# A seven-product scheme for the down projection of two token blocks

## The chip, the cores and the metric

The kernel runs on one core of a Trainium2 chip. The metric is the device time of one execution in microseconds (us); the median of three runs is given. The engines are TensorE (PE: matmuls; PEld: its weight loads), VectorE (DVE), ScalarE (ACT), GpSimd (POOL) and SyncE (SP), whose queue issues nearly all DMAs.

## The reference

One decoder layer over 2048 tokens with model width 1024: a modulated norm, an input projection, forgetting attention beside a state-space group, an output projection with a gated residual; then a gated MLP with a causal convolution of width 3. Only the MLP matters here:

```python
D_FF = 2816
h = rmsnorm(x, g_ffn[l]) * (1.0 + sc_f) + sh_f
gate_pre, val = jnp.split(h @ w_up[l], 2, axis=-1)
gate_pre = causal_dwconv(gate_pre, conv_w[l], conv_b[l])
y = (jax.nn.silu(gate_pre) * val) @ w_down[l]
x = x + gt_f * y
return rmsnorm(x, g_final)
```

All inputs and outputs are float32.

## The kernel before

Tokens are worked on in four blocks of 512 (TB). Tensors lie transposed: 128 channels on the partitions, tokens along the free dimension. The hidden width of 2816 is cut into 22 rows of 128 (NFF), the model width into 8 tiles of 128. A float32 product is made of three matmuls in a reduced format: every operand is split into a high part (a cast on ScalarE, line 77 for weights) and a low part (a subtraction on VectorE, line 78), and high x high, low x high and high x low are added up in a PSUM bank.

Blocks 0 and 1 go through the MLP one by one. Blocks 2 and 3 go together, and for them the up projection already uses a seven-product scheme (Winograd's form of Strassen's): `up_pair(i)` computes row i of the gate and of the value for both blocks at once. The 2 x 2 shape is made of the two halves of the model width (inner), gate and value (outputs) and the two blocks. Its weight combinations s1 to s4 are computed on POOL (lines 1353 to 1358), its operands are in SBUF from earlier on, and its seven products accumulate in the PSUM banks X and Y (two buffers each) and Z (one). In the program's order: X takes b11, Y takes b21, Z takes t1; X then takes t2 on top, Z takes b22, X takes t3, a second Y takes t4. In between, copies (L1385, L1387, L1389, L1395) and additions (L1386, L1391, L1396, L1399) take the running sums out to gs (gate) and vz (value), which have two buffers each. Then come the convolution and SiLU over both blocks (L1403 to L1409, on cvt, gs and vz), and the result, 128 x 1024, is split into ah (L1412) and al (L1413) and written to DRAM by two DMAs (L1415). The tiles cvt, ah and al share four buffers with the tag "row".

`down_pair(b)` is then run for block 2 and for block 3. It goes twice over four outputs d with four accumulators in PSUM, over the 22 rows in the groups FFG = (6, 6, 5, 5). The parts of the first group's activations are loaded into buffers of the tag h (L1434), those of the other groups into tiles of their own (L1437), x1 (the residual) into the yt tiles (L1451). Weights come for each block anew through two raw buffers and three buffers for each of the parts. The matmuls are L1472 to L1474. After the last group each output is scaled by tf, added to x1 (L1424), squared (L333) and summed (L334). Block 2's norm (its scalings are L1492) is put six steps into block 3. In block 3 the last group's last four outputs are made in two halves of 256 tokens, each followed by `finish_last`: sums over the channels, an inverse root in small VectorE operations (L166 to L176), scalings on VectorE (L1516) and POOL (L1514), and the output's DMAs.

The order of the instructions in each engine's queue is set before the run by a planner with a cost model: among instructions whose inputs and buffers are ready in its model, the one that comes first in the program goes first. `tc.issue_after` puts instructions of a block behind a given one on its queue, and `tc.high_priority` moves a block forward. A pool hands out a buffer of a tag once the last reader of its previous content is done. Opening a pool where another was closed waits tile by tile.

Of the kernel before, what the change touches and what calls it, by code (L numbers as in the profile page):

```python
# [12 lines left out]
F32 = mybir.dt.float32  # L13
F32R = mybir.dt.float32r
# [3 lines left out]
ALU = mybir.AluOpType  # L18
# [28 lines left out]
NSC = 2  # L47

# [63 lines left out]
def hybrid_layer(ctx, tc, x, c_t, w_ada, b_col, gains, w_flat, bf_row, a_re, a_im, log_dt,  # L112
# [88 lines left out]
    act_d = [dt(f"act{i}", [2, P, 2, TB]) for i in range(NFF)]  # L201
# [1136 lines left out]
    def up_pair(i, ops, ups):  # L1338
# [71 lines left out]
        ah = row_pool["row"].tile([P, n], F32R, name="ah", tag="row", bufs=4)  # L1410
        al = row_pool["row"].tile([P, n], F32R, name="al", tag="row", bufs=4)
        A.copy(ah, vz)  # L1412
        V.tensor_tensor(out=al, in0=vz, in1=ah.bitcast(F32), op=ALU.subtract)  # L1413
        for j, a in enumerate((ah, al)):
            (A if i == NFF - 1 else Q).dma_start(act_d[i][:, :, j, :].rearrange("b p n -> p b n"),  # L1415
                        a.rearrange("p (b n) -> p b n", b=2).bitcast(F32))

    def down_pair(b, ap, dps, misc, tail):

        sq = sq_acc()  # L1420
        act, yt, step = [], [], 0

        def evict(d, ps, ts, eng):
            V.scalar_tensor_tensor(out=yt[d][:, ts], in0=ps[:, ts], scalar=mod["tf"][:, d : d + 1], in1=yt[d][:, ts],  # L1424
                                   op0=ALU.mult, op1=ALU.add)
            sum_squares(sq, d == 0, yt[d][:, ts], ts, eng)

        def load_act(g):
            c0 = sum(FFG[:g])
            for c in range(c0, c0 + FFG[g]):  # L1430
                if g == 0:
                    act.append(h_parts())
                    for j, t in enumerate(act[-1]):
                        Q.dma_start(t.bitcast(F32), act_d[c][b % 2, :, j])  # L1434
                else:
                    t = ap.tile([P, 2, TB], F32R, name="act", tag=f"act{c}", bufs=1)
                    Q.dma_start(t.bitcast(F32), act_d[c][b % 2])  # L1437
                    act.append((t[:, 0], t[:, 1]))

        load_act(0)  # L1440
        for half in range(2):
            ds = range(4 * half, 4 * half + 4)
            pss = {d: dps.tile([P, 512], F32, name="acc_ps", tag="acc", bufs=4) for d in ds}
            c0 = 0
            for g, n in enumerate(FFG):
                last = g == len(FFG) - 1
                if g == 2:
                    with tc.issue_after(weights.last.ins):
                        for d in ds:
                            t = ap.tile([P, TB], F32, name="yt", tag="yt", bufs=8)  # L1450
                            Q.dma_start(t, x1_d[b][d])  # L1451
                            yt.append(t)
                cut = tail and last and half == 1
                ws = {}
                for p in range(2 if cut else 1):
                    ts = slice(p * 256, (p + 1) * 256) if cut else slice(0, TB)
                    for d in ds:
                        if d not in ws:
                            so, sn = dn_slots[g][d]
                            own = [ap.tile([P, sn], F32R, name=f"w_{nm}", tag=f"cut_{nm}{d}", bufs=1)  # L1460
                                   for nm in ("hi", "lo")] if cut else (None, None)
                            ws[d] = weights.split(weights.raw(so, sn), sn, *own)
                        wh, wl = ws[d]
                        if half == 0 and d == ds[3] and not last:
                            with tc.issue_after(weights.last.ins):
                                load_act(g + 1)
                        for c in range(n):
                            ah, al = (t[:, ts] for t in act[c0 + c])
                            a, bb = wh[:, c * P : (c + 1) * P], wl[:, c * P : (c + 1) * P]
                            st = g == 0 and c == 0  # L1470
                            sp_ = c == n - 1 and (last or tail and half == 1 and g == len(FFG) - 2)
                            T.matmul(pss[d][:, ts], lhsT=a, rhs=ah, start=st, stop=False, skip_group_check=cut)  # L1472
                            T.matmul(pss[d][:, ts], lhsT=a, rhs=al, start=False, stop=False, skip_group_check=cut)
                            T.matmul(pss[d][:, ts], lhsT=bb, rhs=ah, start=False, stop=sp_, skip_group_check=cut)  # L1474
                            step += 1
                            if step == 6 and norm_late:
                                norm_late.pop()()
                        if last:
                            evict(d, pss[d], ts, V)
                    if cut:  # L1480
                        with tc.high_priority():
                            finish_last(b, yt, sq, p, misc)
                c0 += n
# [252 lines left out]
```

## Time and profile before

| | us |
|---|---|
| median of 3 runs | 2645.68 |
| lowest and highest | 2643.41, 2648.35 |
| the profiled execution | 2644.54 |
| its span, first to last instruction | 2642.8 |

Row 1 to row 21 of `up_pair` fill the time up to 2374.3 us, and the two calls of `down_pair` the rest. All times of the trace count from the start of the span. In the page's list of groups a row shows the line, the engine, the operation, output <- inputs, shape and count, then the busy time and the mean duration in ns, then the idle time of the engine before these instructions and what ended it. A timeline row starts with its start and its duration in us. In a row of waits stand: who waited for whom, us in total, times, the longest.

### The profile page before, as it was taken

What the parts mean: (1) busy time and instruction counts of PE and PEld (TensorE: products, weight loads), DVE (VectorE), ACT (ScalarE), POOL (GpSimd) and SP (SyncE); (2) the same over time, 40 slices, a digit from 0 to 9 for tenths busy, and PEclk for the clock granted to TensorE, in tenths of its full rate; (3) what the DMA queues carried; (4) which work ended last, traced back from release to release, by engine and by line L of the source; (5) the groups of instructions that cost most, each with busy time, mean ns of one, the idle gap of its engine ahead of it and who ended that gap; (6) DMA issues with size and microseconds to landing.
All of it is one profiled execution on the core that took longest, in us unless ns stands there. A gap on an engine that the chain in (4) does not pass through costs nothing.

```text
span 2642.8 us, 35640 instructions
## 1 busy us (share of the span) xinstructions
PE 2552.0 (97%) x12343; PEld 2066.4 (78%) x12343; DVE 1934.6 (73%) x3568; ACT 1237.3 (47%) x2056; POOL 184.2 (7%) x146
## 2 busy tenths in 40 slices
PE   6999999998999999999999999999989999999997
PEld 3888777887788888888778877888768888887876
DVE  7989588966887878886877767676598778773343
ACT  3423255553564545564645555565544444442222
POOL 0001000000000000000000000000034334320000
PEclk8999999999999999999999999999999999999999
DMA  8586987667466565655656555556623232346563
GB/s 300 165 267 209 293 266 211 201 195 239 144 205 214 188 200 165 204 176 201 198 184 223 178 191 172 184 173 248 223 91 120 102 121 97 118 162 246 173 229 100
DMA packets 265925, 500.63 MB, mean 189 GB/s; under 512 B 27120, under 2 KB 111984, under 8 KB 265744
## 3 DMA queue, kind: packets, MB, share of 16 engines
q1 hardware_dynamic: 263920, 493.10, 56.9%
q0 software_dynamic: 1280, 4.20, 0.4%
q8 instruction: 98, 1.61, 0.3%
q10 hardware_dynamic: 544, 1.05, 0.1%
q14 instruction: 83, 0.68, 0.1%
HBM read 371.17 MB, written 127.01 MB: 189 GB/s over the span
## 4 chain that ended last, share of the span: by engine, by line
PE 76%; DMA 8%; DVE 8%; issue 4%; ACT 1%; SPq 1%; POOL 0%; ACTq 0%; DVEq 0%; POOLq 0%
PE ff_ps L1248 18%; PE up_x L1371 7%; PE ff_ps L1222 6%; PE up_y L1371 4%; PE up_z L1371 4%; PE ff_ps L1280 3%; PE ff_ps L1282 3%; PE ff_ps L1281 3%; DMA wada<-in_w_ada 3%; PE o_ps L1008 2%; PE o_ps L1012 2%; PE qs_ps L462 2%; PE vq_ps L462 2%; DMA w_raw<-in_w_flat 2%; PE proj_ps L429 2%
## 5 line engine op out<-in xcount | busy, mean ns | idle before, releaser
L78 DVE TENSOR_TENSOR w_lo<-w_raw,w_hi 128x1024 fp32r<-128x1024 f32 (+2 forms) x219 | 235.6, 1077 | 204.7 <-ACT w_hi L77 202.7
L77 ACT CAST w_hi<-w_raw 128x1024 fp32r<-128x1024 f32 (+2 forms) x219 | 203.0, 929 | 359.1 <-DMA w_raw<-in_w_flat 109.0
L1248 PE MATMUL ff_ps<-h_lo,w_hi 128*128 128x512 f32 x704 | 279.4, 397 | 0.9 <-DVE h_lo L381 0.8
L1248 PE MATMUL ff_ps<-h_hi,w_lo 128*128 128x512 f32 x704 | 279.6, 397 | 0.0
L1248 PE MATMUL ff_ps<-h_hi,w_hi 128*128 128x512 f32 x704 | 279.2, 399 | 0.0
L999 DVE TENSOR_TENSOR pl<-pf,ph 128x512 fp32r<-128x512 f32 (+1 forms) x320 | 194.8, 618 | 18.6 <-ACT ph L998 17.6
L998 ACT CAST ph<-pf 128x512 fp32r<-128x512 f32 (+1 forms) x320 | 177.9, 569 | 61.5 <-PE o_ps L1008 55.6
L1007 DVE TENSOR_TENSOR acc<-acc,pf 128x512 f32<-128x512 f32 (+2 forms) x264 | 159.2, 604 | 28.6 <-ACT pf L997 26.0
L1248 PEld LDWEIGHTS ff_ps<-h_lo,w_hi 128*128 128x128 f32 x704 | 133.3, 189 | 29.8 <-DVE h_lo L381 1.4
L997 ACT ACTIVATE pf<-sc_ps 128x512 f32<-128x512 f32 (+2 forms) x184 | 98.4, 539 | 122.4 <-PE sc_ps L988 73.7
L1248 PEld LDWEIGHTS ff_ps<-h_hi,w_lo 128*128 128x128 f32 x704 | 133.1, 189 | 28.8
L1248 PEld LDWEIGHTS ff_ps<-h_hi,w_hi 128*128 128x128 f32 x704 | 133.2, 189 | 28.7 <-issue 0.2
L107 ACT CAST w_hi<-w_raw 128x1024 fp32r<-128x1024 f32 (+2 forms) x100 | 96.4, 964 | 104.1 <-PE ff_ps L1222 42.2
L1281 PE MATMUL ff_ps<-act_lo,w_hi 128*128 128x512 f32 x352 | 139.5, 397 | 0.0
L1280 PE MATMUL ff_ps<-act_hi,w_hi 128*128 128x512 f32 x352 | 139.3, 398 | 0.2 <-ACT rt L368 0.2
L1282 PE MATMUL ff_ps<-act_hi,w_lo 128*128 128x512 f32 x352 | 139.4, 397 | 0.0
L949 DVE TENSOR_REDUCE mx<-sc_ps 128x1 f32<-128x512 f32 (+2 forms) x164 | 97.5, 599 | 50.2 <-PE sc_ps L944 25.5
L1008 PE MATMUL o_ps<-ph,vv 128*128 128x512 f32 (+1 forms) x320 | 120.8, 378 | 1.7 <-ACT ph L998 1.7
L1371 PE MATMUL up_x<-hh,w_hi 128*128 128x512 f32 x352 | 112.7, 400 | 6.1 <-DVE hh L378 4.4
L1012 PE MATMUL o_ps<-pl,vv 128*128 128x512 f32 (+2 forms) x312 | 116.2, 374 | 0.9 <-DVE pl L999 0.9
L1472 PE MATMUL acc_ps<-act,w_hi 128*128 128x512 f32 (+1 forms) x276 | 105.0, 380 | 3.1 <-ACT w_hi L77 2.5
L1474 PE MATMUL acc_ps<-act,w_lo 128*128 128x512 f32 (+1 forms) x276 | 104.5, 380 | 0.4
(581 smaller groups left out, 6719.6 us busy)
## 6 DMA issues: line engine op xcount, KB each, us to landing
w_raw<-in_w_flat SPq DMA_DIRECT2D x193, 512.0 KB
w_lo<-wlo SPq DMA_DIRECT2D x68, 512.0 KB
wlo<-w_lo SPq DMA_DIRECT2D x52, 512.0 KB
w_raw<-in_w_flat SPq DMA_DIRECT2D x64, 384.0 KB
kb<-kb SPq DMA_DIRECT2D x80, 256.0 KB
vv<-v SPq DMA_DIRECT2D x80, 256.0 KB
w_raw<-in_w_flat SPq DMA_DIRECT2D x64, 320.0 KB
act<-act SPq DMA_DIRECT2D x32, 512.0 KB
```

Of the source, the lines that this page charges most:

```text
L77: nc.scalar.copy(hi[:, :n], raw[:, :n])
L78: nc.vector.tensor_tensor(out=lo[:, :n], in0=raw[:, :n], in1=hi[:, :n].bitcast(F32), op=ALU.subtract)
L998: A.copy(ph[:, cs], pf[:, cs])
L999: V.tensor_tensor(out=pl[:, cs], in0=pf[:, cs], in1=ph[:, cs].bitcast(F32), op=ALU.subtract)
L1007: eng.tensor_tensor(out=acc[j][:, cs], in0=acc[j][:, cs], in1=pf[:, cs], op=ALU.add)
L1008: T.matmul(o_ps[:, cs], lhsT=vt[:, i, :], rhs=ph[:, cs], start=first, stop=False)
L1012: T.matmul(o_ps[:, cs], lhsT=vt[:, i, :], rhs=pl[:, cs], start=False, stop=(b > 0 and ch == b - 1 and i == 3))
L1248: T.matmul(ps, lhsT=lt, rhs=rt, start=(n == 0), stop=(n == 23))
L1280: T.matmul(ps, lhsT=a, rhs=ah[:, ts], start=(c == 0), stop=False)
L1281: T.matmul(ps, lhsT=a, rhs=al[:, ts], start=False, stop=False)
L1282: mark[0] = T.matmul(ps, lhsT=bb, rhs=ah[:, ts], start=False, stop=(c == n - 1))
L1371: mark[0] = T.matmul(ps, lhsT=lt, rhs=rt, start=(first and n == 0), stop=(n == 11), skip_group_check=not first)
```

## The change

`down_pair` for two blocks becomes `down_both`. Rows 0, 1 (FIRST) and 18 to 21 (LAST) stay direct products, for both blocks. Rows 2 to 17 form eight row pairs in the groups JOINT of two, three and three pairs. For a group and a pair of outputs the 2 x 2 shape is: even and odd row (inner), the two outputs, the two blocks. Seven products replace eight, with the weight sums s1 to s4 made on VectorE from the raw weights of the two outputs, and with eight additions from PSUM into the outputs y, which are in SBUF for both blocks from the start. They are begun by the FIRST rows (copied out with the scale tf on ScalarE); x1 is added later.

The operands of the seven products (b11, b21, t1, t2, b22, t3, t4) are made in `up_pair`: an even row of a joint pair stores its block 2 part as b11 and keeps vz; the odd row makes four differences and six operands. Each operand is split into both parts in one tile and written with one DMA of 512 KB. In the down stage, operands, activations and x1 go through 27 buffers (ROOM: 9 of h, 6 on the right side, 12 in the pool "act"), filled in order of use as buffers come free, with a cap that rises from step to step (`state["room"]`).

```diff
+RING = 6
+RINGL = 12
+NHP = 9
+ROOM = NHP + RING + RINGL
+STEP = 3
+FIRST = (0, 1)
+LAST = (18, 19, 20, 21)
+JOINT = ((1, 2), (3, 4, 5), (6, 7, 8))
+KINDS = ("b11", "b21", "t1", "t2", "b22", "t3", "t4")
...
+        if i in act_d:
...
+            return
+        def operand(kind, f):
+            o = row_pool["row"].tile([P, 2, TB], F32R, name="op", tag="row", bufs=4)
+            A.copy(o[:, 0], f)
+            V.tensor_tensor(out=o[:, 1], in0=f, in1=o[:, 0].bitcast(F32), op=ALU.subtract)
+            Q.dma_start(op_d[i // 2][kind], o.bitcast(F32))
+        def comb(a, b, to):
+            V.tensor_tensor(out=to, in0=a, in1=b, op=ALU.subtract)
+            return to
+        if i % 2 == 0:
+            operand("b11", va)
+            even[0] = vz
+            return
+        b11, b12 = even[0][:, 0:TB], even[0][:, TB : 2 * TB]
+        c13, c24 = (row_pool["row"].tile([P, 2, TB], F32, name="c", tag="row", bufs=4) for _ in range(2))
+        t1 = comb(b12, b11, c13[:, 0])
+        t3 = comb(vb, b12, c13[:, 1])
+        t2 = comb(vb, t1, c24[:, 0])
+        t4 = comb(va, t2, c24[:, 1])
+        for kind, f in (("b21", va), ("t1", t1), ("t2", t2), ("b22", vb), ("t3", t3), ("t4", t4)):
+            operand(kind, f)
...
+        for d in range(8):
+            w = weights.split(w_cols(0, n, d), n * P)
+            for b in (2, 3):
+                ps = bank(next(banks))
+                plain(ps, w, first[b])
+                t = rp.tile([P, TB], F32, name="yt", tag=f"yt{b}{d}", bufs=1)
+                y[b].append(t)
+                A.activation(t, ps, AF.Copy, scale=tf[:, d : d + 1])
+            state["room"] = min(state["room"] + STEP, 4 + 7 * len(JOINT[0]))
+            with tc.issue_after(weights.last.ins):
+                fill()
...
+                s12, s1, s2 = pair("s12")
+                s_op(s1, a21, a22, ALU.add)
+                s_op(s2, s1, a11, ALU.subtract)
+                w12 = weights.split(s12, 2 * n * P)
+                s43, s4, s3 = pair("s43")
+                s_op(s4, a12, s2, ALU.subtract)
+                s_op(s3, a11, a21, ALU.subtract)
+                w43 = weights.split(s43, 2 * n * P)
+                A.copy(hv, a22)
+                V.tensor_tensor(out=lv, in0=a22, in1=hv.bitcast(F32), op=ALU.subtract)
+                w22 = (hi, lo)
...
+                X, Y, Z = bank("x"), bank("y"), bank("z")
+                product(X, wa, 0, 2 * P, "b11")
+                product(Y, wa, P, 2 * P, "b21")
+                add(2, d1, X)
+                product(Z, w12, 0, P, "t1")
+                add(2, d1, Y)
+                add(3, d2, Z)
+                product(X, w12, n * P, P, "t2", False)
+                add(3, d1, X)
+                product(Z, w43, 0, P, "b22", False)
+                add(3, d1, Z)
+                product(X, w43, n * P, P, "t3", False)
+                add(2, d2, X)
+                add(3, d2, X)
+                Y2 = bank("y")
+                product(Y2, w22, 0, P, "t4")
+                add(2, d2, Y2)
+                if g == len(JOINT) - 1 and dp:
+                    for d in range(4):
+                        add_x1(*((2, d), (2, d + 4), (3, d))[dp - 1])
...
+                with tc.high_priority():
+                    norm_late.append(norm_of(2, y[2], sq, misc))
+            else:
...
+                norm_late[0](range(8))
...
```

In the last pass of a group (dp = 3) the buffers of each product's operands are given to the next group's loads. Block 2's scalings now stand in the program ahead of block 3's two halves. X, Y and Z have two PSUM banks each in the down stage.

More of the change, by code (lines that the diff above doesn't have):

```diff
@@ L200, in hybrid_layer @@
     x1_d = {b: [dt(f"x1_{b}_{d}", [P, TB]) for d in range(8)] for b in (2, 3)}
-    act_d = [dt(f"act{i}", [2, P, 2, TB]) for i in range(NFF)]
+    act_d = {i: dt(f"act{i}", [2, P, 2, TB]) for i in FIRST + LAST}
+    op_d = {j: {k: dt(f"op{j}{k}", [P, 2, TB]) for k in KINDS} for js in JOINT for j in js}
     off = 0
@@ L1409, in up_pair @@
         V.scalar_tensor_tensor(out=vz, in0=t, scalar=0.5, in1=vz, op0=ALU.mult, op1=ALU.mult)
[L1410 to L1434, printed above, removed]
-                else:
[L1436 to L1447, printed above, removed]
-                    with tc.issue_after(weights.last.ins):
[L1449 to L1483, printed above, removed]
-        if not tail:
-            ps = misc()
-            token_sums(ps, sq, 0, 4)
-            r = rsqrt_mean(ps[:, 0:4], 4, D)
-            def norm():
-                rt = spread(r, misc)
-                for d in range(8):
-                    V.scalar_tensor_tensor(out=yt[d], in0=yt[d], scalar=gain[:, 24 + d : 25 + d], in1=rt,
-                                           op0=ALU.mult, op1=ALU.mult)
-                    Q.dma_start(out[b, d], yt[d])
-            norm_late.append(norm)
@@ new lines, in up_pair @@
+        if i in act_d:
+            ah = row_pool["row"].tile([P, n], F32R, name="ah", tag="row", bufs=4)
+            al = row_pool["row"].tile([P, n], F32R, name="al", tag="row", bufs=4)
+            A.copy(ah, vz)
+            V.tensor_tensor(out=al, in0=vz, in1=ah.bitcast(F32), op=ALU.subtract)
+            for j, a in enumerate((ah, al)):
+                (A if i == NFF - 1 else Q).dma_start(act_d[i][:, :, j, :].rearrange("b p n -> p b n"),
+                            a.rearrange("p (b n) -> p b n", b=2).bitcast(F32))
+            return
@@ L1498, in hybrid_layer, with norm_of, norm @@
+    def norm_of(b, yt, sq, misc):
+        ps = misc()
+        token_sums(ps, sq, 0, 4)
+        r = rsqrt_mean(ps[:, 0:4], 4, D)
+        rt = spread(r, misc)
+        def norm(ds):
+            for d in ds:
+                V.scalar_tensor_tensor(out=yt[d], in0=yt[d], scalar=gain[:, 24 + d : 25 + d], in1=rt,
+                                       op0=ALU.mult, op1=ALU.mult)
+                Q.dma_start(out[b, d], yt[d])
+        return norm
     norm_late = []
@@ L1639, in hybrid_layer @@
             pass
-    up_ctx.close()
     late_ctx.close()
     vq_ctx.close()
+    ring_ctx = ExitStack()
+    rp = opened(ring_ctx, "ring", bufs=RING, side="right")
+    up_ctx.close()
     fp_ctx.close()
@@ L1645, in hybrid_layer @@
     with ExitStack() as stk:
+        stk.enter_context(ring_ctx)
         ap = opened(stk, "act", bufs=1)
@@ L1651, in misc @@
             return dps.tile([P, 512], F32, name="misc_ps", tag="misc", bufs=2)
-        for b in (2, 3):
-            down_pair(b, ap, dps, misc, b == 3)
+        down_both(ap, rp, dps, misc)
     hp_ctx.close()
```

144 lines of the change are left out of this document (added).

## The prediction

> **What bounds the kernel now.** I read the page's busy line first, then stretches of the end of the kernel (the activations' up rows, then the down stage), then the chain of waits and the groups of instructions inside those stretches. Columns of a stretch: its length, then PE, weight load, DVE, ACT and POOL busy, granted clock, DMA share, GB/s.
>
> ```profile
> PE 2552.0 (97%) x12343; PEld 2066.4 (78%) x12343; DVE 1934.6 (73%) x3568; ACT 1237.3 (47%) x2056; POOL 184.2 (7%) x146
> 1990.00:2340.00 350.00, 349.88 (x1504) 282.28 (x1503) 267.98 (x271) 161.25 (x198) 130.12 (x73) 1.00 0.31 110
> 2374.30:2629.00 254.70, 250.30 (x1135) 203.21 (x1134) 91.16 (x139) 65.52 (x93) 0.00 (x0) 1.00 0.55 188
> 2384.00:2394.00 10.00, 9.65 (x42) 7.44 (x41) 2.78 (x3) 2.04 (x3) 0.00 (x0) 1.00 0.89 324
> 2394.00:2404.00 10.00, 9.73 (x42) 7.60 (x41) 1.92 (x2) 1.67 (x2) 0.00 (x0) 1.00 1.03 412
> 2404.00:2414.00 10.00, 8.05 (x34) 5.92 (x33) 1.61 (x2) 1.45 (x2) 0.00 (x0) 1.00 0.59 217
> 2424.00:2434.00 10.00, 9.24 (x39) 6.89 (x38) 2.82 (x4) 2.82 (x4) 0.00 (x0) 1.00 0.27 85
> 2616.00:2628.50 12.50, 11.96 (x101) 11.76 (x99) 7.57 (x25) 3.97 (x9) 0.00 (x0) 1.00 0.00 1
> ```
>
> TensorE bounds both stages: 349.88 of 350 us in the up rows, 250.30 of 254.7 in down, at full clock. DVE has 77% in the up rows but 36% in down. The 4.4 us that PE stands idle in down lie mostly in 2384 to 2434 (0.35 + 0.27 + 1.95 + 0.76 = 3.3 us), where the activations of later rows come in at up to 412 GB/s. One product of twelve matmuls gives the price of a matmul, from the chain of waits:
>
> ```profile
> 2223.91 2.80 PE up_z L1371 x12
> 2226.70 2.79 PE up_x L1371 x12
> 2229.49 2.78 PE up_y L1371 x12
> 2232.28 2.78 PE up_z L1371 x12
> ```
>
> 2.79 / 12 = 0.2325 us for 128x128 by 512.
>
> **The change, part by part.**
>
> *Matmuls removed.* Rows 2 to 17 for both blocks cost 16 rows x 8 outputs x 2 blocks x 3 = 768 matmuls; seven products over 8 row pairs and 4 output pairs cost 8 x 4 x 7 x 3 = 672. The six direct rows keep their 288. 96 matmuls fewer, all on the path: 96 x 0.2325 = **-22.3 us**. Nothing else is a gain, except PE's 4.4 us of idle time, if the new loads avoid it.
>
> *Up rows: more work on DVE.* Groups of 2000 to 2340, then two rows of the steady state as one stretch:
>
> ```profile
> L1413 DVE TENSOR_TENSOR al<-vz,ah 128x1024 fp32r<-128x1024 f32 x18 | 22.1, 1226 | 16.8 <-ACT ah L1412 16.8
> L78 DVE TENSOR_TENSOR w_lo<-v_raw,w_hi 128x512 fp32r<-128x512 f32 x17 | 14.5, 852 | 0.0
> L1412 ACT CAST ah<-vz 128x1024 fp32r<-128x1024 f32 x18 | 18.9, 1050 | 36.8 <-DVE vz L1409 36.8
> L77 ACT CAST w_hi<-v_raw 128x512 fp32r<-128x512 f32 x17 | 10.6, 623 | 22.2 <-PE up_y L1371 22.2
> 2199.00:2238.10 39.10, 39.10 (x169) 31.58 (x169) 29.72 (x31) 17.91 (x22) 14.05 (x8) 1.00 0.30 108
> ```
>
> A pair of rows loses two 1024-wide splits (2 x 1.226 on DVE, 2 x 1.050 on ACT) and gets four subtractions and seven 512-wide splits: DVE 11 x 0.852 - 2.45 = +6.9 us, so 36.6 of 39.1; ACT 7 x 0.623 - 2.10 = +2.3, so 20.2 of 39.1. ACT has room. DVE fits on the mean, but ten of the eleven come after the odd row and fall into the next even row, which then holds 14.9 + 10 x 0.852 - 1.2 = 22.1 us of work in 19.55; it gives 2.6 us of it to the row behind. Each pair also writes seven 512 KB operands in place of four, all through SP, at a DMA share of 0.30: covered, unless a weight load stands behind a write that waits for DVE; then up to the delay of that split.
>
> One wait is new. The even row's vz (two buffers) must live until the odd row's subtractions, and vz of the row after that needs its buffer, at L1387, the copy that empties bank Z.
>
> ```profile
> 2226.43 1.71 DVE L1409 SCALAR_TENSOR_TENSOR vz<-cvt,vz 128x1024 f32<-128x1024 f32 x1
> 2228.07 0.68 DVE L78 TENSOR_TENSOR w_lo<-v_raw,w_hi 128x512 fp32r<-128x512 f32 x1
> 2229.14 0.58 ACT L1387 COPY vz<-up_z 128x512 f32<-128x512 f32 x1
> ```
>
> L1387 stands just behind L1409 already. The two subtractions that read the old vz add about 1.4 us, so Z would be empty near 2231 in place of 2229.7; its next product starts at 2232.28 with another (up_y) in between. So it is covered here by 1.3 us; where a DVE operation slips in ahead, PE waits. The odd row's operands also hold two of the four "row" buffers while the other two hold the differences, which delays the next row's convolution, with cvt; nothing on PE waits for that directly. I take 0.4 us per pair, +3 us for eight pairs; ends 0 and +16 (0 and 2 us per pair, the lower because PE waits 0.12 us in 350 us now, the upper the cover plus one 0.7 us split). A gain is excluded: PE has no idle time there to give.
>
> That rests on the mean of 0.852; the row varies with POOL:
>
> ```profile
> 2244.14 1.15 DVE L78 TENSOR_TENSOR w_lo<-v_raw,w_hi 128x512 fp32r<-128x512 f32 x1
> 2242.45 2.29 POOL L1358 TENSOR_TENSOR s<-w_raw,v_raw 128x512 f32<-128x512 f32 x1
> ```
>
> The same 512-wide split takes 0.68 us with POOL idle and 1.15 beside a POOL operation. If all eleven met POOL: 11 x 1.15 - 2.45 = 10.2, 39.9 us in a pair of 39.1, 0.8 x 8 = 6.4 us lost. [...]
>
> *Start of down.* Four operands of rows 0 and 1, then 14 of the first joint group stream in. Before, buffers of h came free early:
>
> ```profile
> 2355.86 0.32 SPq L1434 DMA_DIRECT2D h_hi<-act  x1
> 2370.93 0.38 SPq L1434 DMA_DIRECT2D h_hi<-act  x1
> ACT w_hi L77 <- DMA w_raw<-in_w_flat: 78.0, 21, 10.3
> ```
>
> 14 x 0.524 MB and 2.1 MB of weights at 412 GB/s take 22.9 us; the direct rows give 96 x 0.2325 = 22.3 us, and the last operand is wanted 8 us after that. So it fits, if weights aren't caught behind operands, as they were 21 times before (up to 10.3 us). Idle time stays as it was: 0 net, ends -3.3 (none) and +6 (most of one such wait). [...]
>
> *Joint stage.* Groups of the down stage:
>
> ```profile
> L78 DVE TENSOR_TENSOR w_lo<-w_raw,w_hi 128x768 fp32r<-128x768 f32 x30 | 28.6, 957 | 52.7 <-ACT w_hi L77 52.7
> L1424 DVE SCALAR_TENSOR_TENSOR yt<-acc_ps,mod_tf,yt 128x512 f32<-128x512 f32 x12 | 9.0, 747 | 8.4 <-PE acc_ps L1474 8.4
> L334 DVE TENSOR_TENSOR sq_acc<-sq_acc,sq 128x512 f32<-128x512 f32 x10 | 6.9, 686 | 0.0
> L1492 DVE SCALAR_TENSOR_TENSOR yt<-yt,gain,rt 128x512 f32<-128x512 f32 x8 | 5.4, 748 | 1.3 <-ACT rt L368 1.3
> L1424 DVE SCALAR_TENSOR_TENSOR yt<-acc_ps,mod_tf,yt 128x256 f32<-128x256 f32 x8 | 3.9, 484 | 4.2 <-PE acc_ps L1474 4.1
> L334 DVE TENSOR_TENSOR sq_acc<-sq_acc,sq 128x256 f32<-128x256 f32 x8 | 3.4, 425 | 2.7 <-ACT sq L333 2.6
> ```
>
> An output pair of a two-pair group takes PE 42 x 0.2325 = 9.76 us. DVE: eight additions x 0.747, four weight sums (256 wide) x 0.425, three splits x 0.68, one x 0.43: 10.2 us of durations. Neighbours overlap by nearly 0.1 us (2226.43 + 1.71 is 2228.14, the next started at 2228.07), so some 9 of 9.76: no reserve. In a three-pair group PE takes 14.65 and DVE 8 x 0.747 + 4 x 0.56 + 3 x 0.957 + 0.56 = 11.7 (0.56 for 384 wide lies between the rows for 256 and 512); the last group has four additions of x1 more in three passes, 14.4, about 13 with the overlap. Further, both raw weight tiles of a pass are needed until its last split, so the second tile of the next pass is fetched some 4.5 us into a pass (the last split's buffer comes free after two products, 2.8, and the split follows) and wanted at 9.76 + 2.8 = 12.5, with two sums and a split in between. SP itself is no bound: a three-pair group issues 21 operands (a third of them as two) and some 12 weight pieces, 40 x 0.38 = 15 us in 58.6. Two-pair group **+3 us** (0 to +10: four passes of 0.4 plus a late fetch of 2). Other groups and the direct rows of block 2: **+1** (0 to +6, half a us a pass).
>
> *Tail.*
>
> ```profile
> 2627.57 0.28 PE L1473 MATMUL acc_ps<-act,w_hi 128*128 128x256 f32 x1
> 2627.69 0.28 PE L1474 MATMUL acc_ps<-act,w_lo 128*128 128x256 f32 x1
> 2629.74 1.66 DVE L1516 SCALAR_TENSOR_TENSOR yt<-yt,gain,misc_ps 128x256 f32<-128x256 f32 x4 [0.35 <-ACT rt L1509]
> 2631.32 0.15 DVE L166 TENSOR_SCALAR rs_v<-misc_ps 128x2 f32<-128x2 f32 x1
> 2634.18 0.16 DVE L176 SCALAR_TENSOR_TENSOR rs_y<-rs_t,rs_y 128x2 f32<-128x2 f32 x1
> ```
>
> After the last product the first half's four scalings delay the second half's inverse root (2631.32 to 2634.34, 3 us). A 256-wide matmul follows the one before after 0.12 us. Now a half lasts 4 x 12 x 0.12 = 5.8 us in place of 60 x 0.12 = 7.2, and block 2's eight scalings (8 x 0.748 = 6 us), which lay in the middle of the stage, stand in this last phase. DVE there: eight splits 5.4, four additions with squares 5.7, scalings 6, root 3, half 0 3.6, its finish 4.7: 28 us against PE's 23. Some goes ahead in block 2's rows: **+3 us**, ends -1 (all of it ahead) and +7.
>
> **Sum.** -22.3 + 3 + 0 + 3 + 1 + 3 = -12.3. The profiled execution took 2644.54 (span 2642.8), 1.1 under the median of 2645.68; 2632.2 in its terms, **2633** against the median. 0.2% (5.3 us) is what a measurement of this kernel can tell from no change: faster means under 2640.4.
>
> **Rivals.**
> - *Full gain.* Up rows and passes lose nothing, the stream starts clean: 2645.7 - 22.3 - 3.3 = 2620. For it: 64% of DVE free in down. Against: the even row with 22.1 us of DVE work in 19.55.
> - *POOL beside all new DVE work.* 6.4 in place of 3 in the up rows: 2637. [...]
> - *Weights become the bound of the joint stage.* Each of twelve passes waits 1 us for its second raw tile: 12 in place of 4, 2641, no change that can be told. For it: ACT's 78 us of waits for raw weights; against: two splits of reserve.
> - *Slower: Z waits for vz.* If L1387 in each even row comes a whole product late (2.79), 8 x 2.79 = 22.3 in place of 3: 2653. It decides from 2.6 us a pair (20.6 / 8, which takes 15.3 of gain to 5.3 of loss). For it: L1387 already sits behind L1409, and that row's DVE is full. Against: the product between, 1.3 us of cover.
>
> **How the numbers follow.** Forecast 0.47 (own range 2625 to 2640), full gain 0.17, POOL 0.08, weights 0.14, Z 0.14. Faster: 0.47 + 0.17 + 0.08 less a little at the edge, 0.70; same 0.15; slower 0.15. The range, 2619 to 2649, leaves out the worse half of Z and a little below the full gain.
>
> **What the changed profile would show.** Up rows still 19.55 us long, or rows with PE waiting for vz L1387 or a late w_lo; DVE near 94% there. PE's count down by 96. The two-pair group as 39 us, or longer with waits for w_lo or raw weights. From last product to end 15 us, or 18. Wrong would be PE idle above 10 us in up, or ACT waiting for w_raw in every pass.

## The result

| | before | after |
|---|---|---|
| median of the runs compared, us | 2647.01 (2643.41 to 2648.87) | 2628.37 (2624.23 to 2632.36) |
| after to before | | 0.9931, 95% interval 0.991 to 0.9952 |
| the profiled execution, us | 2644.54 | 2632.36 |
| its span, us | 2642.8 | 2630.6 |

18.6 us are gone by the medians; the forecast was 12.3. The profiled executions differ by just 12.2, and that number misleads: the one of after is the slowest of its four. The page's busy line of after, then whole stages of after and of before as single stretches (length, then PE, weight load, DVE, ACT and POOL busy, granted clock, DMA share, GB/s):

```profile
PE 2542.1 (97%) x12235; PEld 2057.4 (78%) x12235; DVE 2050.5 (78%) x3808; ACT 1256.8 (48%) x2120; POOL 182.7 (7%) x146
0.00:1930.40 1930.40, 1872.05 (x9344) 1521.11 (x9345) 1485.19 (x3028) 967.73 (x1704) 25.38 (x53) 0.98 0.64 206
1990.00:2340.00 350.00, 349.88 (x1506) 282.99 (x1505) 299.40 (x345) 176.24 (x239) 123.35 (x74) 1.00 0.41 146
2379.30:2611.56 232.26, 228.78 (x1022) 183.59 (x1020) 174.93 (x286) 69.09 (x112) 0.00 (x0) 1.00 0.62 218
2611.60:2630.60 19.00, 2.65 (x12) 1.95 (x12) 11.30 (x43) 2.81 (x7) 4.85 (x7) 0.57 0.44 148
```

```profile
0.00:1924.70 1924.70, 1861.90 (x9343) 1511.89 (x9344) 1484.85 (x3029) 968.17 (x1706) 25.21 (x53) 0.98 0.64 207
2374.30:2627.97 253.67, 250.20 (x1134) 203.08 (x1132) 90.42 (x135) 65.11 (x92) 0.00 (x0) 1.00 0.55 188
2628.00:2642.80 14.80, 1.64 (x8) 1.00 (x8) 7.40 (x25) 1.16 (x3) 4.86 (x7) 0.66 0.43 142
```

Everything before the up rows is the same code, yet it took 5.7 us longer in after's execution (1930.4 against 1924.7), with PE busy 10.2 us longer for as many matmul records (9344 and 9343). Over the fourteen profiled executions of this document it ended between 1921.5 and 1930.4. So the change is read in its own stages, cut at the first product of the up rows, the start of their last product, the last product of all, and the end:

| us | before | after | difference | forecast |
|---|---|---|---|---|
| up rows | 449.6 | 448.9 | -0.7 | +3 |
| down to the last product | 253.67 | 232.26 | -21.4 | -22.3 + 0 + 3 + 1 = -18.3 |
| tail | 14.83 | 19.04 | +4.2 | +3 |
| sum | | | -17.9 | -12.3 |

That is close to the -18.6 of the medians, but in part by chance: six profiled executions here share after's joint stage, and after's down is the shortest of them (232.3; the other five 233.4 to 234.7, 234.2 on the mean, for a reason that the last run below shows). With 234.2 the sum is -16.0. The interval of the medians, 12.7 to 23.8 us less, holds both. Of before there is one profiled execution only.

In the up rows nothing on PE waits from 1990 on, with DVE at 299.4 of 350 us (86%; before 268.0); in the 60 to 65 us ahead of that PE stands idle for 10 to 11 us in both kernels. In down PE waits in two places, in the two-pair group and at the last change of group. The waits of PE and of ACT from 2374 on:

```profile
PE acc_x L1611 <- ACT w_hi L86: 1.3, 1, 1.3
PE acc_x L1611 <- DVE w_lo L87: 1.0, 1, 1.0
ACT w_hi L86 <- DMA w_raw<-in_w_flat: 38.2, 10, 12.3
```

The longest of ACT's ten waits for a raw weight tile stands at the change from the second to the third group. SP's queue and ACT there (start, duration):

```profile
2500.97 0.32 SPq L1497 DMA_DIRECT2D h_hi<-op6t  x1
...
2512.62 0.32 SPq L1497 DMA_DIRECT2D h_lo<-op8t  x1
2513.35 2.30 SPq L1473 DMA_DIRECT2D w_raw<-in_w_flat  x4
2519.18 0.83 ACT L86 CAST w_hi<-w_raw 128x768 fp32r<-128x768 f32 x1 [12.28 <-DMA w_raw<-in_w_flat]
```

The weights of the next group's first pass are issued behind 21 loads of that group's operands: nine from 2494.5 on, then twelve, of which the first and the last are shown, over 11.7 us, as PE frees their buffers one by one. The two raw buffers were free by then: their last readers on VectorE, a weight sum and a split, ended at 2499.7 and 2507.5. So at this place it is the order in SP's queue that makes the weights late. From 2514.8 to 2525.7 PE loses 3.2 us, and 1.6 us in the two-pair group (2422 to 2426), counted as the time between the starts of neighbouring matmuls beyond 0.2325 us, in gaps of over 0.3 us.

The tail, DVE's rows:

```profile
2606.29 5.38 DVE L1680 SCALAR_TENSOR_TENSOR yt<-yt,gain,rt 128x512 f32<-128x512 f32 x8
2611.59 0.42 DVE L344 TENSOR_TENSOR sq_acc<-sq_acc,sq 128x256 f32<-128x256 f32 x1
2613.49 0.15 DVE L175 TENSOR_SCALAR rs_v<-misc_ps 128x2 f32<-128x2 f32 x1
2618.15 0.16 DVE L175 TENSOR_SCALAR rs_v<-misc_ps 128x2 f32<-128x2 f32 x1 [1.28 <-PE misc_ps L352]
```

Block 2's eight scalings go as one piece ahead of half 0's last square. Half 0's inverse root (2613.49) begins 1.9 us after the last product's end at 2611.56; half 1's follows it. In before the same root was in its second step 3 us ahead of that end (2627.97):

```profile
2624.98 0.17 DVE L168 TENSOR_SCALAR rs_i<-rs_v 128x2 int32<-128x2 int32 x1
```

### The profile page after: what moved, and what is told of

Read it like the earlier page. It is cut to its first block, busy times and chain, and to the rows that moved or that the text cites. A ratio compares the mean times of both kernels' runs of the same rounds, so it can differ in the third digit from the quotient of the medians.

```text
span 2630.6 us, 35879 instructions
## 1 busy us (share of the span) xinstructions
PE 2542.1 (97%) x12235; PEld 2057.4 (78%) x12235; DVE 2050.5 (78%) x3808; ACT 1256.8 (48%) x2120; POOL 182.7 (7%) x146
## 3 DMA queue, kind: packets, MB, share of 16 engines
q10 hardware_dynamic: 544, 1.05, 0.1%
## 4 chain that ended last, share of the span: by engine, by line
PE 81%; DVE 9%; DMA 5%; ACT 2%; issue 2%; SPq 1%; POOL 0%; DVEq 0%; POOLq 0%; ACTq 0%
PE ff_ps L1258 19%; PE ff_ps L1232 7%; PE up_x L1381 6%; PE up_y L1381 4%; PE up_z L1381 4%; PE ff_ps L1290 3%; PE ff_ps L1292 3%; PE ff_ps L1291 3%; PE o_ps L1018 2%; PE qs_ps L472 2%; PE o_ps L1022 2%; PE acc_x L1611 2%; PE vq_ps L472 2%; PE acc_z L1611 2%; PE acc_y L1611 2%
## 5 line engine op out<-in xcount | busy, mean ns | idle before, releaser
L86 ACT CAST w_hi<-w_raw 128x1024 fp32r<-128x1024 f32 (+4 forms) x187 | 173.1, 927 | 264.3 <-DMA w_raw<-in_w_flat 62.2
L87 DVE TENSOR_TENSOR w_lo<-w_raw,w_hi 128x1024 fp32r<-128x1024 f32 (+4 forms) x187 | 200.9, 1075 | 72.7 <-ACT w_hi L86 67.0
L1009 DVE TENSOR_TENSOR pl<-pf,ph 128x512 fp32r<-128x512 f32 (+1 forms) x320 | 194.7, 618 | 19.4 <-ACT ph L1008 18.3
L116 ACT CAST w_hi<-w_raw 128x1024 fp32r<-128x1024 f32 (+2 forms) x100 | 96.5, 965 | 107.9 <-PE ff_ps L1232 45.2
L1381 PE MATMUL up_z<-hh,w_hi 128*128 128x512 f32 x308 | 98.6, 401 | 1.4 <-ACT vz L1397 0.9
L86 ACT CAST w_hi<-s 128x1024 fp32r<-128x1024 f32 (+2 forms) x66 | 62.1, 944 | 78.4 <-DVE s L1582 30.7
```

Source lines behind the costliest of these rows:

```text
L86: nc.scalar.copy(hi[:, :n], raw[:, :n])
L87: nc.vector.tensor_tensor(out=lo[:, :n], in0=raw[:, :n], in1=hi[:, :n].bitcast(F32), op=ALU.subtract)
L1009: V.tensor_tensor(out=pl[:, cs], in0=pf[:, cs], in1=ph[:, cs].bitcast(F32), op=ALU.subtract)
L1381: mark[0] = T.matmul(ps, lhsT=lt, rhs=rt, start=(first and n == 0), stop=(n == 11), skip_group_check=not first)
```

## The experiments

Every run was timed beside the kernel before on the same chip; ratios are to that. "Down" and "tail" are the stages above, from each run's own trace.

**The matmuls: the seventh product's work put back.** The t4 product of every pass runs twice, so 96 matmuls are added and nothing else.

```diff
-                product(Y2, w22, 0, P, "t4")
+                product(Y2, w22, 0, P, "t4", free=False)
+                product(Y2, w22, 0, P, "t4")
```

> The changed kernel with the last product (t4) of every pass run twice into the same bank, the second run starting the bank anew: 8 x 4 x 3 = 96 matmuls of 512 more, no other work. Theory 1 (TensorE still sets the joint stage, so the 96 matmuls that the scheme saves were worth their full price): 96 x 0.2325 = 22.3 us longer than the changed kernel in the stage of down, a time near the kernel before, 2647 to 2652. Rival (VectorE, the weights or the operand stream set the passes): the added product fills time in which PE waits, under 15 us longer.

Measured 2643.23, ratio 0.9993 (0.9981 to 1.0004): the whole gain is gone. Down became 247.63, 15.4 longer than after's and 13.0 longer than in the last run below. That is neither theory alone: less than the 22.3 of the first, and at the rival's limit. Down lost its idle time:

```profile
2374.70:2622.33 247.63, 247.62 (x1118) 202.44 (x1116) 176.46 (x287) 69.28 (x112) 0.00 (x0) 1.00 0.57 203
```

PE is busy in 247.62 of 247.63 us. The gaps on PE, which in after's down come to 6.7 us more than here with all small ones counted, are filled: 22.3 - 6.7 = 15.6. So PE's count of matmuls sets the floor of the stage, and after's waits come from passes that are now too short for what feeds them.

**The up rows: DVE's reserve.** Each operand's low part is subtracted twice (seven more 512-wide subtractions a pair).

```diff
-            V.tensor_tensor(out=o[:, 1], in0=f, in1=o[:, 0].bitcast(F32), op=ALU.subtract)
+            for _ in range(2):
+                V.tensor_tensor(out=o[:, 1], in0=f, in1=o[:, 0].bitcast(F32), op=ALU.subtract)
```

> The changed kernel with the low part of each of the 56 operands in the up rows computed twice: per row pair 7 subtractions of 0.68 us more on VectorE, 33.4 + 4.8 = 38.2 us of work in 39.1 us. Theory 1 (TensorE is covered there with slack for VectorE; what VectorE does late is taken up by the two buffers of each tile): the up rows stay at 19.55 us, change under 3 us. Rival (the up rows stand at VectorE's edge, as the prediction's +3 us had it): at least 1 us per pair, 8 us and more in the up rows.

Measured 2637.72, ratio 0.9976 (0.9964 to 0.9989). The up rows took 457.3, 8.4 more than after, 1.05 a pair. The same 350 us, and what PE waited for in 1990 to 2350:

```profile
1990.00:2340.00 350.00, 345.30 (x1472) 275.33 (x1472) 335.27 (x390) 169.03 (x232) 124.76 (x71) 1.00 0.40 142
PE up_x L1381 <- ACT w_hi L86: 2.6, 3, 0.9
PE up_z L1381 <- ACT vz L1397: 1.4, 4, 0.8
```

That is the rival's figure. At 96% DVE the up rows do lose time, and a part of it in the wait that the prediction feared, up_z for vz; at after's 86% they lose none. DVE held 33.4 us a pair in after (299.4 / 350 x 39.1) and some 38.2 here; the edge lies between.

**The joint stage: how the weights come late.** First more and smaller groups, so more changes of group:

```diff
-JOINT = ((1, 2), (3, 4, 5), (6, 7, 8))
+JOINT = ((1, 2), (3, 4), (5, 6), (7, 8))
```

> The eight row pairs in four groups of two in place of two, three, three: 14 operands a group, so with 27 buffers 13 of the next group's 14 are loaded ahead, where before 15 of the third group's 21 had to come during the last pass of the second. The same matmuls, but 16 passes of 9.76 us in place of 4 of 9.76 and 8 of 14.65, and VectorE's work per pass about 9 of 9.76 us. Theory 1 (the 3 us that PE waits around 2515 us are the operand stream at a group's change): these waits go, 2 to 3 us less there. Rival (what costs is VectorE's and the weights' pace in a two-pair pass, 1.6 us in the first group): 12 more such passes, 3 to 8 us longer.

Measured 2654.95, ratio 1.0044 (1.0031 to 1.0057), slower than before; down 263.45, 31.2 more than after. PE's and ACT's waits, then the whole stage and three stretches at the first of the long waits:

```profile
PE acc_x L1611 <- ACT w_hi L86: 23.5, 3, 9.3
ACT w_hi L86 <- DMA w_raw<-in_w_flat: 58.2, 9, 15.3
2372.60:2636.05 263.45, 236.36 (x1022) 188.46 (x1020) 200.26 (x351) 72.12 (x128) 0.00 (x0) 0.95 0.56 193
2456.50:2465.90 9.40, 0.45 (x2) 0.01 (x1) 2.07 (x3) 0.35 (x1) 0.00 (x0) 0.72 0.81 319
2465.90:2475.90 10.00, 9.68 (x33) 7.75 (x34) 7.36 (x14) 2.43 (x5) 0.00 (x0) 0.75 0.18 52
2475.90:2485.90 10.00, 10.00 (x45) 8.06 (x44) 9.21 (x17) 2.27 (x4) 0.00 (x0) 1.00 0.27 71
```

Three waits of 23.5 us, one at each change of group, and PE busy for 7.6 us more (236.36 against 228.78 for as many matmuls): the sum is the 31.2. The 7.6 go with the granted clock: 0.95 over the stage (1.00 in after), 0.75 in the 10 us behind a wait of 9.3, 1.00 in the next 10. Ahead of the first wait SP issues 17 operand loads from 2442.5 on, and then the weights, whose buffers had been free since 2446.9 and 2451.8; the cast waits for them another 10.7 us:

```profile
2454.89 13.87 SPq L1473 DMA_DIRECT2D w_raw<-in_w_flat  x3
2465.55 0.62 ACT L86 CAST w_hi<-w_raw 128x512 fp32r<-128x512 f32 x1 [15.32 <-DMA w_raw<-in_w_flat]
```

So Theory 1 had the right place, but in smaller groups its wait grew in place of going. Why no run tests; a pass is shorter here, which leaves less time for the loads in front of the weights.

Is it SP's order alone? The joint passes' raw weights issued from POOL's queue instead:

```diff
-            ahead.append([w_cols(2 * js[0], 2 * len(js), d) for d in (2 * dp, 2 * dp + 1)])
+            ahead.append([w_cols(2 * js[0], 2 * len(js), d, G) for d in (2 * dp, 2 * dp + 1)])
```

> The raw weights of the joint groups are issued from POOL's queue, which is idle there, in place of SP's, where they stand behind the operand loads; the same bytes, the same buffers. Theory 1 (PE's waits around 2422 and 2514 us come from weight loads that stand behind a burst of operand loads in SP's queue): these waits go, the stretch from the up rows' end to the last product falls from 232 us to 227 to 229. Rival A (the two raw buffers, still in use by the splits, hold the loads back): no change there. Rival B (the DMA engines themselves are full during the bursts): no change, or the operands come later and PE waits for them instead.

Measured 2642.68, ratio 0.9994 (0.9982 to 1.0006); down 246.05, 13.8 more than after. The 227 to 229 us of Theory 1 did not come. The loads now wait on POOL's queue for their buffers, but PE's waits have another cause for the most part:

```profile
POOL w_raw L1473 <- ACT w_hi L86: 92.8, 10, 15.0
PE acc_z L1613 <- ACT w_hi L86: 7.3, 3, 2.6
2504.49 1.41 DVE L1525 SCALAR_TENSOR_TENSOR yt<-acc_x,mod_tf,yt 128x512 f32<-128x512 f32 x2 [2.28 <-PE acc_x L1613]
2505.82 0.55 DVE L1584 TENSOR_TENSOR s<-w_raw 128x384 f32<-128x384 f32 x1
```

At the change to the third group the raw tiles were issued as soon as their buffers were free, at 2487.07 and 2494.30, and had landed by 2501.3. But in the planner's order VectorE first does additions that wait for PE (2.1 and 2.3 us idle), and the first weight sum comes at 2505.82; PE then waits for it from 2507.3. PE's gaps of 2.7, 2.0, 2.7 and 3.4 us at 2397, 2409, 2507 and 2522 are all of this kind; those of 1.5 and 2.3 at 2393 and 2445 follow a landing.

The edit also moved the operand loads: they are put behind the last weight load of SP's queue, and as the joint weights left it, SP issued nine loads of the second group from 2383.5 to 2392.0, ahead of the first joint pass (in after they start at 2406.5, some 5 us into that pass). The first two weight tiles landed after 7.4 and 7.8 us, many later ones after 3. So this run changed three things, the queue of the weights, the order of the operand loads and the order on VectorE, and does not separate queue from buffers.

Next, the raw buffers: each joint pass's second tile gets two buffers of its own (room for them from s43, which keeps one).

```diff
-            raw = wpool.tile([P, WSLOT], F32, name="w_raw", tag="w_raw", bufs=2)
+            raw = ap.tile([P, 768], F32, name="w_raw", tag="w_own", bufs=2) if own else wpool.tile([P, WSLOT], F32, name="w_raw", tag="w_raw", bufs=2)
...
-                    t = ap.tile([P, 6 * P], F32, name=nm, tag=nm, bufs=2)
+                    t = ap.tile([P, 6 * P], F32, name=nm, tag=nm, bufs=2 if nm == "s12" else 1)
```

> Four raw weight buffers in place of two for the joint groups (two of them in another pool; one of the buffers of a weight sum is given up for room), all loads on SP as before. Rival A of the run with POOL's queue (the two raw buffers hold the loads back): the stretch from the up rows' end to the last product falls from 232 to 227 to 229 us. The queue theory: the loads can be issued a pass earlier and so get ahead of the burst in part, 0 to 3 us less.

Measured 2622.64 (2618.65 to 2637.14), ratio 0.9935 (0.9914 to 0.9957); down 226.9, 5.4 less than after. The loads start up to a pass earlier, and the planner's order in SP's queue changed with them: of the third group's first pass one tile is issued at 2477.38, ahead of the 21 operand loads, and the other at 2495.58, ahead of the last six, where after had both behind all 21. That four buffers bring the loads in time is shown; how much of it is the buffers themselves and how much the new order is not:

```profile
ACT w_hi L86 <- DMA w_raw<-in_w_flat: 9.0, 4, 5.6
2372.90:2599.80 226.90, 226.28 (x1022) 184.08 (x1020) 173.63 (x286) 69.45 (x112) 0.00 (x0) 1.00 0.63 223
```

ACT's 38.2 us of waits are 9.0, and PE's are all but gone. With the 22.3 alone down would be 231.4; the other 4.5 are the idle time of before (3.5 us) and 1 us that I have not traced. The median's interval is too wide to hold this 5.4 apart from after; the stage shows it.

**The tail.** First block 2's scalings moved from DVE to ACT (gain) and POOL (inverse root):

```diff
-                V.scalar_tensor_tensor(out=yt[d], in0=yt[d], scalar=gain[:, 24 + d : 25 + d], in1=rt,
-                                       op0=ALU.mult, op1=ALU.mult)
+                A.activation(yt[d], yt[d], AF.Copy, scale=gain[:, 24 + d : 25 + d])
+                G.tensor_tensor(out=yt[d], in0=yt[d], in1=rt, op=ALU.mult)
```

> Block 2's eight final scalings are taken from VectorE: ScalarE multiplies by the gain, POOL by the inverse root, with a buffer of their own for the latter. Theory 1 (the tail is longer by 4.2 us because the eight scalings, 5.4 us in one piece on VectorE, stand ahead of block 3's additions and squares): last product to end 15 us in place of 19, total 3 to 5 us less than the changed kernel. Rival (the tail is longer because a half is only 5.8 us of PE and the inverse roots of both halves pile up, or POOL's work slows VectorE as much): under 1.5 us less.

Measured 2628.68, ratio 0.9943 (0.9922 to 0.9963); tail 20.67, longer by 1.6. The piece is gone from DVE, but DVE's small operations beside it grew:

```profile
2600.85 10.73 POOL L1684 TENSOR_TENSOR yt<-yt,rt 128x512 f32<-128x512 f32 x8 [260.51 <-ACT rt L1679]
2605.39 1.07 DVE L177 TENSOR_SCALAR rs_i<-rs_v 128x2 int32<-128x2 int32 x1
2610.38 1.21 DVE L185 SCALAR_TENSOR_TENSOR rs_y<-rs_t,rs_i 128x2 f32<-128x2 f32 x1
2611.91 0.14 DVE L183 TENSOR_TENSOR rs_t<-rs_y 128x2 f32<-128x2 f32 x1
```

Half 0's root began 1.5 us ahead of the last product's end, but five of its operations took 0.92 to 1.21 us in place of 0.16 while POOL ran, 4.8 us in all. That run swapped one delay for another and decides nothing on the piece itself. Next, half 1's weights kept from block 2's pass, which takes four splits and their loads out of the last phase:

```diff
-                w = weights.split(w_cols(LAST[0], n, d), n * P)
+                if d < 4:
+                    w = weights.split(w_cols(LAST[0], n, d), n * P)
+                else:
+                    t = ap.tile([P, 2, TB], F32R, name="ring", tag="ring", bufs=RINGL)
+                    w = own[d] = weights.split(w_cols(LAST[0], n, d), n * P, t[:, 0], t[:, 1])
```

> The split weights of outputs 4 to 7 of rows 18 to 21 are made once, in block 2's pass, and kept for block 3's two halves: four loads, four casts and four subtractions of 0.69 us fewer in the last phase. Theory 1 (the tail is VectorE's backlog in the last phase): last product to end falls by 2 to 4 us from 19, to 15 to 17. Rival (the tail's length is the chain sums, inverse root, scaling, output of each half, with little queueing): under 1 us.

Measured 2632.03, ratio 0.9953 (0.9935 to 0.997); tail 18.74, 0.3 less. The eight scalings still went as one piece, at 2605.08. Both edits at once, this one and the weights on POOL's queue:

> The joint groups' raw weights on POOL's queue and the kept split weights together. If both theories hold their gains add up: 232 to 228 before the last product, tail 19 to 16, total 6 to 8 us less than the changed kernel, 0.9900 to 0.9910 of the kernel before. If the tail isn't VectorE's backlog, 3 to 4 us less; if neither holds, as the changed kernel.

Measured 2642.36, ratio 0.9996 (0.9986 to 1.0006); down 245.68, tail 19.02: as with POOL's queue alone (246.05, 19.75), so kept weights have no gain to give there either. Then the piece itself was left out:

```diff
-                V.scalar_tensor_tensor(out=yt[d], in0=yt[d], scalar=gain[:, 24 + d : 25 + d], in1=rt,
-                                       op0=ALU.mult, op1=ALU.mult)
```

> Left out: block 2's eight scalings by gain and inverse root; its y is written as it is. In the changed kernel the eight (5.38 us in one piece at 2606.29) stand on DVE ahead of half 0's last squares. Theory 1, that this piece delays half 0's inverse root and with it the first half's scalings and the end: the tail (last product to end) goes from 19.04 to 15 us (14 to 16.5), the total falls by 3 to 5 us against the changed kernel. Theory 2, that half 0's own chain after shorter passes, not the piece, sets the tail: 18 us or more, total within 1.5 us of the changed kernel.

The tail became 15.32. DVE's rows that answer to those of after; the last product ended at 2610.18:

```profile
2608.44 0.16 DVE L175 TENSOR_SCALAR rs_v<-misc_ps 128x2 f32<-128x2 f32 x1
...
2612.89 0.16 DVE L175 TENSOR_SCALAR rs_v<-misc_ps 128x2 f32<-128x2 f32 x1 [0.82 <-PE misc_ps L352]
```

Half 0's root starts 1.7 us ahead of the last product's end in place of 1.9 behind it: 3.6 of the 3.7 us. So the piece is the cause of the tail's growth. The total, though, was 2627.72, ratio 0.9933 (0.9916 to 0.9951), against 2626.46 for the changed kernel on the same chip (last run below). The profiled executions differ by 3.6 us as the stages say (2627.15 and 2630.73), the medians do not; why is open.

Can the scalings stay and not delay? With four raw buffers, and with a tile of its own for block 2's inverse root, one scaling put behind each of half 1's additions and two behind each half's root:

```diff
-                norm_late[0](range(8))
...
+                        if p == 1:
+                            with tc.issue_after(e.ins):
+                                norm_late[0]((d - 4,))
...
+                    with tc.issue_after(root[0].ins):
+                        norm_late[0]((4 + 2 * p, 5 + 2 * p))
```

> The four raw weight buffers of the earlier run with block 2's scalings spread out: one behind each of half 1's four additions, two behind each half's inverse root. Theory 1 (the piece delays half 0's root): down 227, tail 15.5 (14.5 to 17), total 3 to 4 us under that of the run with four raw buffers alone (2622.6), so 2619. Theory 2 (block 2's long chain to its inverse root stands in the way, since the splits of outputs 4 to 7 fill DVE ahead of it): tail 18 to 19, total 2622 to 2623.

Measured 2623.19, ratio 0.9916 (0.9899 to 0.9934); down 228.4, tail 18.8. Half 0's root began at 2606.32, again 1.7 behind the last product's end (2604.60): VectorE goes without a pause of over 0.5 us from 2597 to 2606, through splits, additions and scalings, and the squares come late again. With the kept weights as well:

> As the run before it, and the split weights of outputs 4 to 7 kept from block 2's pass, so that half 1's four splits (some 2.7 us of DVE) and their loads are gone from the last phase. Theory 1: tail 15 to 16 and down 227, total 8 to 9 us under the changed kernel on this chip, ratio to before 0.990. Theory 2 (the two do not add, as DVE is not what the last phase waits for): tail 18 or more, total as with four raw buffers alone, ratio to before 0.992.

Measured 2623.93, ratio 0.9919 (0.9906 to 0.9933); down 228.03, tail 17.27, 245.3 in all against 251.3 in after, the shortest of all runs. Here the last product ended at 2602.63:

```profile
2601.01 0.16 DVE L177 TENSOR_SCALAR rs_v<-misc_ps 128x2 f32<-128x2 f32 x1 [0.18 <-PE misc_ps L354]
...
2605.68 1.41 DVE L1689 SCALAR_TENSOR_TENSOR yt<-yt,gain,ring 128x512 f32<-128x512 f32 x2
2607.00 0.15 DVE L177 TENSOR_SCALAR rs_v<-misc_ps 128x2 f32<-128x2 f32 x1
```

Half 0's root is in time (1.6 ahead), half 1's is late: two scalings (1.41) stand in front of it, and it starts 4.4 after the last product's end, against 2.7 without any scalings. Neither end of the expectation held: the tail is halfway. And the last measure, the changed kernel once more on this chip:

> The changed kernel itself once more, as the measure for the other three on this chip. If the 18.6 us between the medians came from the change: ratio 0.993 (0.991 to 0.995), down 232 and tail 19. If part of it was the state of that chip: ratio 0.994 to 0.996, nearer to the 17.2 us that the stages show between the two profiled executions.

Measured 2626.46 (2625.52 to 2630.73), ratio 0.9929 (0.9916 to 0.9942): the 18.6 us hold, here 19.0. The version with four raw buffers, spread scalings and kept weights is 2.5 us faster by the medians on this chip, less than the runs of either spread: its stages show a gain of 6.0 us over after's and of 8.5 over those of this run, its times don't yet. In this profile down took 234.67, 2.4 more than in after's. Five microseconds at the change of the last group, in this run and in after:

```profile
2516.00:2521.00 5.00, 3.75 (x10) 2.98 (x11) 4.32 (x7) 0.92 (x2) 0.00 (x0) 0.68 1.04 376
```

```profile
2519.00:2524.00 5.00, 3.93 (x17) 3.07 (x18) 4.54 (x8) 1.10 (x2) 0.00 (x0) 1.00 1.06 386
```

The clock is 0.68 behind the wait for the weights in the one, 1.00 in the other, and over down PE is busy for 230.82 us in the one, 228.78 in the other, for 1022 matmuls in both: 2 us more. After's is the exception: in the four other runs with the same joint stage (DVE's reserve, scalings on POOL, kept weights, scalings left out) PE is busy for 230.0 to 231.0 us of down at a mean clock of 0.99 (after 1.00), and the clock in the 5 us at this place is 0.72 with kept weights and 0.69 with the scalings left out. Against the usual down of 234.2 the four raw buffers are thus worth 7.3 us and not 5.4.

## Why the prediction was right, and where its sizes were off

The likeliest case held: 2628.4 lies 4.6 us under the forecast, inside its own range of 2625 to 2640 and the wide one. The large term, the matmuls, was right by its mechanism; the small ones were off by up to 4 us each, in both directions, and that they left the sum inside the range is in part luck. By its steps, with after's execution as the measure:

- *Matmuls, -22.3.* Right. Putting 96 back filled 6.7 us of waits and took 15.4; with the waits removed by more raw buffers, down came to 226.9, the 22.3 and all idle time.
- *Up rows, +3.* Measured -0.7, so nothing. The working of DVE was 3.2 us a pair too high (36.6 against 33.4): the mean of 0.852 came from splits that often meet POOL (of the 18 in 1990 to 2340 of before, ten beside POOL took 1.08 us on the mean, eight without it 0.68), where the new operations take 0.71 on the mean (the split groups of 1990 to 2340 are below). That is 1.6 of the 3.2; the rest lies in older rows, such as the splits of the weight sums, whose mean fell from 1.528 to 1.282 us in the same 350 us, for a reason that no run tests. And the cover of 1.3 us at Z held. The step that failed is the 0.4 us a pair, taken between 0 and 2 with no row that called for more than 0. The wait itself exists, but only appeared with 4.8 us more of DVE work a pair (0.8 us at most).

```profile
L1433 DVE TENSOR_TENSOR op<-c,op 128x512 fp32r<-128x512 f32 x32 | 24.0, 749 | 24.1 <-ACT op L1432 24.1
L1433 DVE TENSOR_TENSOR op<-vz,op 128x512 fp32r<-128x512 f32 x24 | 16.4, 685 | 0.6 <-ACT op L1432 0.6
```

The feared place in one even row:

```profile
2231.04 1.21 DVE L1419 SCALAR_TENSOR_TENSOR vz<-cvt,vz 128x1024 f32<-128x1024 f32 x1
...
2232.28 0.69 DVE L1437 TENSOR_TENSOR c<-vz 128x512 f32<-128x512 f32 x1
2232.89 0.68 DVE L1437 TENSOR_TENSOR c<-vz,c 128x512 f32<-128x512 f32 x1
2233.34 0.58 ACT L1397 COPY vz<-up_z 128x512 f32<-128x512 f32 x1
2233.49 0.68 DVE L1433 TENSOR_TENSOR op<-vz,op 128x512 fp32r<-128x512 f32 x1
```

L1397 comes right behind the two readers of the old vz; Z's next product started at 2237.24.
- *Start of down, 0 net.* Measured -3.3: PE stood still nowhere from 2379.5 to 2422. Operands stream while the direct rows run, and none of their weights was caught. (The 21 waits of the row from before, taken there for weights caught behind operands, show that ScalarE waited for raw weights, not what stood in front of them.)

```profile
2389.50:2399.50 10.00, 10.00 (x45) 8.11 (x44) 1.66 (x5) 6.44 (x12) 0.00 (x0) 1.00 0.90 317
2409.50:2419.50 10.00, 10.00 (x45) 8.05 (x43) 8.49 (x15) 1.65 (x3) 0.00 (x0) 1.00 0.99 388
2422.00:2432.00 10.00, 8.65 (x35) 6.12 (x34) 8.54 (x16) 2.17 (x4) 0.00 (x0) 1.00 0.72 240
2432.00:2442.00 10.00, 9.99 (x44) 7.60 (x43) 9.34 (x17) 2.49 (x4) 0.00 (x0) 1.00 0.39 124
```

- *Two-pair group, +3.* Measured 1.6, all in its third pass: one split came 1.0 us late. The pass's first raw tile was issued at 2411.10, when its buffer came free (the last sum that reads it ended at 2411.04), but right behind eight operand loads, and it came 9.7 us later, with the DMA at 0.99. The step had the second tile late by its buffer; it was the first one, by its buffer and the burst ahead of it. After that PE was full with DVE at 9.34 of 10 us, so "no reserve" was right and yet cost nothing.
- *Other groups, +1.* Measured 3.2, all of it at one change of group, where the forecast had half a us spread over the passes. The mechanism, the second raw tile fetched late, was named under the two-pair group and for the rival; that the next group's operands would stand in SP's queue in front of both tiles was not. In the five other executions of this stage PE was busy 1.3 to 2.2 us longer than in after's, with a clock of 0.68 to 0.72 behind that wait in three of them; no step had that.
- *Tail, +3.* Measured 4.2, by the mechanism given: block 2's scalings in the last phase. The step put some of them ahead of it; none went.

By the gaps the terms inside down sum to -3.3 + 1.6 + 3.2 = +1.5, by the length of the stage to -21.4 + 22.3 = +0.9. The forecast of 2633 was thus too high by terms that erred in the same direction: up rows 3.7, start 3.3 and two-pair group 1.4, against 2.2 and 1.2 the other way.

Of the rivals, the full gain (2620) failed by the waits in the joint stage and the tail; four raw buffers reach it but for the tail. Weights as the bound of all twelve passes did not come; in the kernel with smaller groups they were the bound at the three changes of group, and that cost more than the change brings. POOL beside all new DVE work (0.71 us on the mean, not 1.15) and Z's wait (PE waits for no vz from 1990 to 2350) were not seen in after's joint rows.

## What to carry to other kernels

When products are taken away from a stage that PE bounds, what was just in time before can come late, as the weights did here (PE lost 1.6 us in the two-pair group and 3.2 at a change of group): check for each stream how many passes ahead its buffers let it run and what stands in front of it in its queue, since here two more raw buffers were worth 5 to 7 us. Another queue for the same loads cost 13.8, for the most part because the order on VectorE changed with it: after such an edit, read the order of every queue before the result is put down to the one that was meant. Work off the path that is moved toward the end (here scalings of 5.4 us) should be laid behind the last chain that the end waits for, not in front of it. And judge by the stage that was changed, in more than one execution: 5.7 us of difference between the profiled executions came from code that was not touched, and the same joint stage took 232.3 to 234.7 us.

## What was not expected of the hardware

- Some waits cost more than their length here. After 9.3 us without a matmul the granted clock was 0.75 over the next 10 us, and down with three such waits (9.3 us the longest, 23.5 together) lost 7.6 us beside them. At the last change of group a wait of 1.4 us behind three gaps of some 0.4 was followed by 0.68 to 0.72 over 5 us in three executions with the same joint stage and by 1.00 in after's. So a lower clock also followed waits far shorter than 9.3 us; what makes after's differ no run here shows.
- VectorE operations on 128x2 elements in SBUF, 0.16 us, took 0.92 to 1.21 while POOL went through 128x512 products of 1.34 us each (10.73 / 8). Those that read PSUM kept their time beside POOL, 0.15 us for the first of the root (2605.21) and 0.47 to 0.48 for a 128x256 addition. The longer durations lie near that of one POOL operation, and the small operations paid no less than larger ones: the sums of squares on 128x256 elements in SBUF, 0.42 to 0.43 us just before, took 0.41 to 0.84 beside the same POOL operations. Why, no run here shows.
